# Stick-breaking attention: the off-diagonal running product over pairs of keys, with the pair products on GpSimd

## The chip, the cores and the metric

The kernel runs on one core of one Trainium2 chip. The metric is device time in microseconds (us). A core has a matrix engine (PE, with its weight loads written PEld), a vector engine (DVE), a scalar engine (ACT), GpSimd (POOL) and a queue engine for transfers (SP). Each engine works through its own list of instructions in order; semaphores tie the lists together.

## The reference

Two layers over a sequence of 2048 positions, width 1024, all float32. Layer 0 pools over neighbouring positions and is all dense products. Layer 1 is the one that the change touches: causal stick-breaking attention with 16 heads of size 64.

```python
def stick_breaking_attention(q, k, v):
    # A[t,s] = beta[t,s] * prod_{s<j<t} (1 - beta[t,j]), beta = sigmoid(q.k / sqrt(d))
    for blk in range(S // Q_BLOCK):
        ...
        mask = s_idx < t_idx
        log_keep = jnp.where(mask, jax.nn.log_sigmoid(-logits), 0.0)
        later = lax.cumsum(log_keep, axis=-1, reverse=True) - log_keep
        a = jnp.where(mask, jnp.exp(jax.nn.log_sigmoid(logits) + later), 0.0)
        outs.append(jnp.einsum('bhts,bhsd->bhtd', a, v[:, :, :L]))
```

For each query t the weights come from a running product of the keep-factors 1 - beta, taken from the query's own position back to the first key. The kernel doesn't form the weights. It forms the running product itself, R[t,s] = the product of the keep-factors from s to t, and multiplies it by the differences of neighbouring rows of V, which gives the same sum.

## The kernel before

The first half (to about 1390 us) does layer 0 and the projections. Q, K and the differences of V go to DRAM split into two parts (a rounded one and the rest), so that PE works at float32 accuracy in its fast format.

The second half is the attention. The sequence is cut into four blocks of 512. The work is a list of slots in the order `for c in 3..0: for h in 0..15: for kc in c..0`: query block c, head h, key block kc. A slot with kc = c is a diagonal slot; the others are off-diagonal, 96 in all. Each slot has four steps j, one for each 128 queries, so query block c = 3 has 256 steps, c = 2 has 192, c = 1 has 128 and c = 0 has 64, and the off-diagonal slots 384. One step runs through these functions:

- `front` (L718, L719): two PE products give the logits of 128 queries against 512 keys in a PSUM tile `psl`. ACT turns them into keep-factors (L722), in one of four fixed buffers `kap`. On a diagonal slot only (j + 1) x 128 keys count, and POOL sets the upper triangle to 1 (L724, a select).
- `scan` (L729): DVE runs the product from the last key to the first, into one of twelve `pp` buffers. It starts from 1 on the diagonal and from the carry of the slot before otherwise, which is the first column of that slot's `pp`.
- `turn` (L743 to L747): PE transposes four 128 x 128 pieces, one from each of the slot's four `pp`, into a PSUM tile `psa` (two buffers). ACT copies it in the rounded format (L746), DVE subtracts to get the rest (L747); both go into a tile `at`.
- `gather` (L755, L756): PE multiplies both parts with the differences of V and adds up in `pso`. At the end of a head `os` takes the result (L760, L761); for every second head ACT adds a bias (L767) and POOL multiplies by the gate (L768).

The main loop is a pipeline written out by hand: at iteration n it issues the turn of step n - 6, the front and the scan of step n, a share of other work, and the gather of step n - 8. A turn needs all four `pp` of its slot.

The other work is a generator of dense products (`piecewise`, L784 to L788), a few PE matmuls per step. Beside c = 3 it is `gate_z`, 32 products, each finished by a DVE multiplication (L825), an ACT sigmoid (L827) and a POOL multiplication (L828). Beside c = 2, 1 and 0 it is `post` of the block before: 8 output projections, each finished on DVE (L849), ACT (L851) and POOL (L852), then 8 gated additions (L871 on ACT, L874 on DVE, L875 on POOL, L876 on DVE); `pair_up` (L804, L805) splits the attention's results. A scheduler may shift instructions within an engine's list; `keep_in_program_order` pins one.

Of the kernel before, what the change touches and what calls it, by code (L numbers as in the profile page):

```python
# [8 lines left out]
F32 = mybir.dt.float32  # L9
F32R = mybir.dt.float32r  # L10
AF = mybir.ActivationFunctionType
ALU = mybir.AluOpType
AX = mybir.AxisListType

P = 128
# [6 lines left out]
W5 = 512  # L22
# [12 lines left out]
def trunk_kernel(ctx, tc, x, p, a_norm, a_w_in, a_w_group, a_scale, a_w_out, kv_norm, w_kv,  # L35
                 k_norm, b_norm, b_w_in, b_q_norm, b_w_out, ple_w, ple_gate_w, out):
    nc = tc.nc
    V, A, G, T = nc.vector, nc.scalar, nc.gpsimd, nc.tensor
# [105 lines left out]
    with ExitStack() as st:  # L144
# [3 lines left out]
        t2 = st.enter_context(tc.tile_pool(name="t2", bufs=2))  # L148
# [516 lines left out]
    with ExitStack() as st:  # L665
        wpair = st.enter_context(tc.tile_pool(name="wpair2", bufs=6))
        t2 = st.enter_context(tc.tile_pool(name="s2", bufs=2))
        kap = st.enter_context(tc.tile_pool(name="kap", bufs=1))
# [7 lines left out]
        zeros = kap.tile([P, 1], F32, name="zeros")  # L676
        V.memset(zeros, 0.0)
        kcount = [0]

        def load_q(c, h):  # L680
            qa = io.tile([P, W5], F32R, tag="io", name="qa")
            qb = io.tile([P, W5], F32R, tag="io", name="qb")
            rows = qd[c][h // 2][h % 2 * HD : (h % 2 + 1) * HD]
            for l in range(2):
                nc.sync.dma_start(out=f(qa)[l * HD : (l + 1) * HD], in_=rows[:, l])
                nc.sync.dma_start(out=f(qb)[(1 - l) * HD : (2 - l) * HD], in_=rows[:, l])
            return qa, qb
# [23 lines left out]
        def front(st, j):  # L711

            w = (j + 1) * P if st["diag"] else W5
            r0 = W5 - w
            ps = psl.tile([P, W5], F32, tag="psl", name="psl")
            qs = slice(j * P, (j + 1) * P)
            (qa, qb), kk = st["q"], st["k"]
            T.matmul(ps[:, :w], qa[:, qs], kk[:, :w], start=True, stop=False)  # L718
            T.matmul(ps[:, :w], qb[:, qs], kk[:, :w], start=False, stop=True)  # L719
            kp = kaps[kcount[0] % NK]  # L720
            kcount[0] += 1
            A.activation(out=kp[:, r0:], in_=ps[:, :w], func=AF.Sigmoid, scale=-1.0)  # L722
            if st["diag"]:
                G.affine_select(out=kp[:, W5 - P :], in_=kp[:, W5 - P :], pattern=[[-1, P]], compare_op=ALU.is_gt,  # L724
                                fill=1.0, base=0, channel_multiplier=1)

            def scan():
                pp = t2.tile([P, W5], F32, tag="pp", name="pp", bufs=12)
                V.tensor_tensor_scan(out=pp[:, r0:][:, ::-1], data0=kp[:, r0:][:, ::-1],  # L729
                                     data1=zeros.to_broadcast([P, w]),  # L730
                                     initial=1.0 if st["diag"] else st["carry"][j], op0=ALU.mult, op1=ALU.add)
                st["carry"][j] = pp[:, r0 : r0 + 1]
                st["a"].append((pp, r0))

            return scan

        def turn(st, kt):

            j0 = kt if st["diag"] else 0
            pt = psa.tile([P, W5], F32, tag="psa", name="psa")  # L740
            for j in range(j0, 4):
                pp, r0 = st["a"][j]
                T.transpose(pt[:, j * P : (j + 1) * P], pp[:, r0 + kt * P : r0 + (kt + 1) * P], ident)  # L743
            at = t2.tile([P, 2, W5], F32R, tag="at", name="at", bufs=3)
            cs = slice(j0 * P, W5)
            A.copy(out=at[:, 0, cs], in_=pt[:, cs])  # L746
            V.tensor_tensor(out=at[:, 1, cs], in0=pt[:, cs], in1=f(at[:, 0, cs]), op=ALU.subtract)  # L747
            st["at"][kt] = at

        def gather(st, kt):  # L750
            cs = slice((kt if st["diag"] else 0) * P, W5)
            if st["diag"] and kt == 0:
                st["o"].append(pso.tile([P, W5], F32, tag="pso", name="pso"))
            po, at, vv = st["o"][0], st["at"].pop(kt), st["v"]
            T.matmul(po[:, cs], vv[:, kt, :], at[:, 0, cs], start=(st["diag"] and kt == 0), stop=False)  # L755
            T.matmul(po[:, cs], vv[:, kt, :], at[:, 1, cs], start=False, stop=(st["last"] and kt == 3))  # L756
            if st["last"] and kt == 3:
                half, os, c, h2 = st["h"] % 2, st["os"], st["c"], st["h"] // 2
                mine, other = slice(half * HD, (half + 1) * HD), slice((1 - half) * HD, (2 - half) * HD)
                A.copy(out=os[mine], in_=po[other])  # L760
                V.tensor_tensor(out=os[mine], in0=po[mine], in1=os[mine], op=ALU.add)  # L761
                if half:
                    zt = t2.tile([P, W5], F32, tag="zt", name="zt", bufs=1)
                    nc.sync.dma_start(out=zt, in_=zd[c][h2])
                    for j in range(4):
                        js = slice(j * P, (j + 1) * P)
                        A.activation(out=os[:, js], in_=os[:, js], func=AF.Identity, bias=ends[c][:, h2, j : j + 1])  # L767
                    G.tensor_tensor(out=os, in0=os, in1=zt, op=ALU.mult)  # L768
                    outs[c].append(os)
# [127 lines left out]
        def beside(c):  # L897

            if c < NSUB - 1:
                yield from post(c + 1)  # L900
                return
            for cz in range(c, -1, -1):
                yield from gate_z(cz)
# [9 lines left out]
        rate = POSTZ / 64.0  # L913
        LAG_T, LAG_G = 6, 8
        done = set()
        ends = {}

        def begin(i):
            c, h, kc = slots[i]
            if kc == c:  # L920
                if h == 1:
                    ends[c] = load_ends(c)
                os = head["os"] if h % 2 else t2.tile([P, W5], F32, tag="os", name="os", bufs=9)
                head.clear()
                head.update(q=load_q(c, h), carry=[None] * 4, o=[], os=os)
            kk, vv = load_kv(kc, h)
            active[i] = dict(head, c=c, h=h, k=kk, v=vv, diag=kc == c, last=kc == 0, a=[], at={})

        for n in range(4 * len(slots) + LAG_G):
            i2, j2 = divmod(n - LAG_T, 4)  # L930
            if 0 <= i2 < len(slots):
                turn(active[i2], j2)
            i, j = divmod(n, 4)
            scan = None
            if i < len(slots):
                c, h, kc = slots[i]
                if j == 0:
                    if i == 0:
                        begin(0)
                    if i + 1 < len(slots):  # L940
                        begin(i + 1)
                scan = front(active[i], j)
            if scan is not None:
                scan()
            owed += rate
            while owed >= 1.0:
                next(filler, None)
                owed -= 1.0
            i3, j3 = divmod(n - LAG_G, 4)
            if 0 <= i3 < len(slots):  # L950
                gather(active[i3], j3)
                if j3 == 3:
                    st3 = active.pop(i3)
                    c3 = st3["c"]
                    if len(outs[c3]) == 8 and c3 not in done:
                        done.add(c3)
                        for _ in filler:
                            pass
                        if c3:
                            filler = beside(c3 - 1)  # L960
                            rate = POST / (64.0 * c3 - 2 * LAG_G)
                            owed = 0.0
# [31 lines left out]
```

## Time and profile before

| what | value |
|---|---|
| median of 3 runs | 2802.99 us (2802.78 to 2803.59) |
| the profiled execution | 2804.4 us, of which its span is 2802.5 us |
| granted PE clock | 0.996 of full speed |
| PE busy | 2735.2 us (98%) |
| DVE busy | 1899.5 us (68%) |
| ACT busy | 1391.6 us (50%) |
| POOL busy | 932.2 us (33%) |

The profile is one execution. A row of its groups has line, engine, operation, tiles written <- read, shape and count, then the busy time in us, the mean in ns of one, and the idle time of the engine before them with what ended it. A row of its timeline has start in us, duration in us, engine, line, operation. A row of its windows gives for each engine the busy time and the number of instructions in one stretch of time. A row of its waits says who waited for whom, the total in us, how often, and the longest. Matmuls are pipelined, and their ends are modelled.

### The profile page before, as it was taken

Reading aid. Unit: us, or ns where it says so; the run is one execution under the profiler, and the core shown is the slowest. Engines: PE = TensorE matmul, PEld = TensorE weight load, DVE = VectorE, ACT = ScalarE, POOL = GpSimd, SP = SyncE. Lnnn points to the kernel's source line nnn. Section 1 sums busy time; section 2 is a strip of 40 time slices with the busy share of each in tenths; the row PEclk is TensorE's granted clock in tenths of the full one; section 3 lists DMA queues with packets and bytes.
Section 4 is the critical chain, followed back from the end, with each engine's and each line's share of the span. In section 5 each row is a group of like instructions: output and inputs, shape, how many; then the busy total and the mean of one; then the engine's idle time right before and its main releaser. Section 6 shows DMA issues by size and latency. Waiting matters only on the chain. (4 is left out here: it accounts for less than half of the span.)

```text
span 2802.5 us, 40461 instructions
## 1 busy us (share of the span) xinstructions
PE 2735.2 (98%) x13731; PEld 2264.3 (81%) x13731; DVE 1899.5 (68%) x2573; ACT 1391.6 (50%) x2801; POOL 932.2 (33%) x949
## 2 busy tenths in 40 slices
PE   8999999999999999999899999999999999999999
PEld 7878888888888888888678888887878778878877
DVE  5655635455355544555299999999999998886642
ACT  5435533445234542345265556556666665554431
POOL 2464337542475425643211111211211122223220
PEclk9999999999999999999999999999999999999999
DMA  8754696647955488455657575555555565668765
GB/s 274 248 180 162 223 321 221 198 161 250 342 172 202 167 270 297 147 183 187 198 183 233 166 224 167 165 170 181 164 168 165 174 188 181 199 183 256 248 204 162
DMA packets 335844, 573.29 MB, mean 205 GB/s; under 512 B 32462, under 2 KB 166638, under 8 KB 335636
## 3 DMA queue, kind: packets, MB, share of 16 engines
q1 hardware_dynamic: 328632, 561.19, 62.2%
q10 hardware_dynamic: 7004, 9.51, 1.1%
q8 instruction: 109, 1.79, 0.3%
q14 instruction: 99, 0.81, 0.1%
HBM read 430.01 MB, written 132.19 MB: 201 GB/s over the span
## 5 line engine op out<-in xcount | busy, mean ns | idle before, releaser
L473 PE MATMUL psd<-wpair,x 128*128 128x512 f32 x2304 | 545.0, 393 | 0.6 <-DVE x L179 0.5
L746 ACT CAST at<-psa 128x512 fp32r<-128x512 f32 (+3 forms) x640 | 333.1, 522 | 407.0 <-PE psa L743 402.0
L729 DVE TENSOR_TENSOR_SCAN pp<-kap,pp,zeros 128x512 f32<-128x512 f32 x384 | 510.8, 1331 | 5.4 <-ACT kap L722 3.2
L473 PEld LDWEIGHTS psd<-wpair,x 128*128 128x128 f32 x2304 | 427.9, 188 | 88.1 <-DVE x L179 1.1
L747 DVE TENSOR_TENSOR at<-psa,at 128x512 fp32r<-128x512 f32 (+3 forms) x640 | 379.1, 594 | 60.1 <-ACT at L746 57.6
L743 PE MATMUL psa<-ident,pp 128*128 128x128 f32 x2176 | 347.1, 275 | 25.7 <-DVE at L747 21.0
L722 ACT ACTIVATE kap<-psl 128x512 f32<-128x512 f32 (+3 forms) x640 | 343.5, 538 | 17.0 <-PE psl L719 8.4
L743 PEld LDWEIGHTS psa<-ident,pp 128*128 128x128 f32 x2176 | 263.5, 141 | 102.8 <-DVE at L747 45.7
L724 POOL TENSOR_SCALAR_AFFINE_SELECT kap<-kap 128x128 f32<-128x128 f32 x256 | 89.6, 351 | 628.0 <-ACT kap L722 522.6
L718 PE MATMUL psl<-kk,qa 128*128 128x512 f32 (+3 forms) x640 | 281.2, 439 | 4.1 <-ACT vr L511 3.4
L729 DVE TENSOR_TENSOR_SCAN pp<-kap,zeros 128x128 f32<-128x128 f32 (+3 forms) x256 | 213.5, 835 | 40.8 <-POOL kap L724 37.4
L756 PE MATMUL pso<-at,vv 128*128 128x512 f32 (+3 forms) x640 | 235.2, 368 | 0.0
L719 PE MATMUL psl<-kk,qb 128*128 128x512 f32 (+3 forms) x640 | 234.7, 367 | 0.0
L755 PE MATMUL pso<-at,vv 128*128 128x512 f32 (+3 forms) x640 | 232.4, 363 | 1.3 <-ACT at L746 1.2
L130 PE MATMUL psd<-xp,wpair 128*128 128x512 f32 x512 | 201.8, 395 | 0.3 <-ACT xp L232 0.3
L131 PE MATMUL psd<-xp,wpair 128*128 128x512 f32 x512 | 200.5, 392 | 0.0
L132 PE MATMUL psd<-xp,wpair 128*128 128x512 f32 x512 | 200.3, 391 | 0.0
L107 POOL TENSOR_TENSOR wpair<-wraw,wpair 128x512 fp32r<-128x512 f32 x99 | 141.1, 1431 | 82.5 <-ACT wpair L105 52.5
L112 DVE SCALAR_TENSOR_TENSOR wpair<-wraw,gains,wpair 128x512 fp32r<-128x512 f32 x192 | 149.0, 796 | 25.8 <-ACT wpair L111 25.0
L111 ACT ACTIVATE wpair<-wraw,gains 128x512 fp32r<-128x512 f32 x192 | 133.9, 718 | 30.9 <-PE psd L473 27.3
L755 PEld LDWEIGHTS pso<-at,vv 128*128 128x128 f32 x640 | 120.4, 188 | 28.2 <-ACT at L746 2.6
L756 PEld LDWEIGHTS pso<-at,vv 128*128 128x128 f32 x640 | 120.5, 188 | 24.9
(206 smaller groups left out, 5408.8 us busy)
## 6 DMA issues: line engine op xcount, KB each, us to landing
kk<-kd SPq DMA_DIRECT2D x320, 128.0 KB
vv<-vd SPq DMA_DIRECT2D x160, 256.0 KB
wraw<-in_w_kv_dram SPq DMA_DIRECT2D x128, 256.0 KB
wpair<-wzd SPq DMA_DIRECT2D x64, 512.0 KB
wpair<-wod SPq DMA_DIRECT2D x64, 512.0 KB
wpair<-wgd SPq DMA_DIRECT2D x64, 512.0 KB
wpair<-wu SPq DMA_DIRECT2D x48, 512.0 KB
wpair<-wi SPq DMA_DIRECT2D x36, 512.0 KB
```

The lines of the kernel that those rows point to most:

```text
L130: T.matmul(ps, wst(units, kt, 0, c0), acts[kt][:, 0], start=(kt == order[0]), stop=False)
L131: T.matmul(ps, wst(units, kt, 0, c0), acts[kt][:, 1], start=False, stop=False)
L473: T.matmul(pss2[i], ck["x2"][kt][:, xh, tk], wst(ws, kt, wh, 0, W5), start=(kt == 0 and xh == 0 and wh == 0), stop=(kt == KT - 1 and wh == 1))
L718: T.matmul(ps[:, :w], qa[:, qs], kk[:, :w], start=True, stop=False)
L719: T.matmul(ps[:, :w], qb[:, qs], kk[:, :w], start=False, stop=True)
L722: A.activation(out=kp[:, r0:], in_=ps[:, :w], func=AF.Sigmoid, scale=-1.0)
L729: V.tensor_tensor_scan(out=pp[:, r0:][:, ::-1], data0=kp[:, r0:][:, ::-1], data1=zeros.to_broadcast([P, w]), initial=1.0 if st["diag"] els ...
L743: T.transpose(pt[:, j * P : (j + 1) * P], pp[:, r0 + kt * P : r0 + (kt + 1) * P], ident)
L746: A.copy(out=at[:, 0, cs], in_=pt[:, cs])
L747: V.tensor_tensor(out=at[:, 1, cs], in0=pt[:, cs], in1=f(at[:, 0, cs]), op=ALU.subtract)
L755: T.matmul(po[:, cs], vv[:, kt, :], at[:, 0, cs], start=(st["diag"] and kt == 0), stop=False)
L756: T.matmul(po[:, cs], vv[:, kt, :], at[:, 1, cs], start=False, stop=(st["last"] and kt == 3))
```

## The change

On off-diagonal slots the running product no longer visits every key. POOL first multiplies neighbouring keep-factors (even key times the odd key above it), which gives 256 products of two keys (P). DVE scans these, from the last pair to the first, and so gets the running product at the even keys. POOL then multiplies each odd key's factor by the running product at the next even key, which fills in the odd keys (O). The `pp` buffers become fixed, two columns longer: a constant 1 in the last column serves as the factor of a pair that holds only the carry, so the scan has 257 entries and writes the carry behind the last key. The P of a step is issued with its front, before its scan; the O of a step is issued one iteration later, after the next front, and pinned there. Diagonal slots keep their scan. Each POOL product has 256 elements for each of 128 partitions, at a step of two elements.

```diff
+        NP = 12
+        pps = [kap.tile([P, W5 + 2], F32, name=f"pp{i}") for i in range(NP)]
+        for pp in pps:
+            G.memset(pp[:, W5 + 1 :], 1.0)
...
+            pp = pps[(kcount[0] - 1) % NP]
+            pp2, m = pp.rearrange("q (n e) -> q n e", e=2), W5 // 2
+            if not st["diag"]:
+                kp2 = kp.rearrange("q (n e) -> q n e", e=2)
+                G.tensor_tensor(out=pp2[:, 0:m, 1], in0=kp2[:, :, 0], in1=kp2[:, :, 1], op=ALU.mult)
+
             def scan():
-                pp = t2.tile([P, W5], F32, tag="pp", name="pp", bufs=12)
-                V.tensor_tensor_scan(out=pp[:, r0:][:, ::-1], data0=kp[:, r0:][:, ::-1],
-                                     data1=zeros.to_broadcast([P, w]),
-                                     initial=1.0 if st["diag"] else st["carry"][j], op0=ALU.mult, op1=ALU.add)
+                if st["diag"]:
+                    V.tensor_tensor_scan(out=pp[:, r0:W5][:, ::-1], data0=kp[:, r0:][:, ::-1],
+                                         data1=zeros.to_broadcast([P, w]), initial=1.0, op0=ALU.mult, op1=ALU.add)
+                else:
+                    V.tensor_tensor_scan(out=pp2[:, :, 0][:, ::-1], data0=pp2[:, :, 1][:, ::-1],
+                                         data1=zeros.to_broadcast([P, m + 1]), initial=st["carry"][j],
+                                         op0=ALU.mult, op1=ALU.add)
+                    odd.append(lambda: tc.keep_in_program_order(G.tensor_tensor(
+                        out=pp2[:, 0:m, 1], in0=kp2[:, :, 1], in1=pp2[:, 1:, 0], op=ALU.mult)))
...
                 scan = front(active[i], j)
+            while odd:
+                odd.pop(0)()
             if scan is not None:
                 scan()
```

1 line of the change is left out of this document (added).

## The prediction

> **What bounds the kernel now.** I read the page, then the windows by stage, then the timeline of one step, then the waits. The profiled execution took 2804.4 us and its span is
>
> ```profile
> span 2802.5 us, 40461 instructions
> ```
>
> so 1.9 us lie around the span; the runs' median, 2802.99 us, is 1.4 us under it. I work in differences and put them on the median. About 0.2% (5.6 us) is the least that a measurement of this kernel can tell from no change.
>
> The change acts in the attention part alone. I cut the trace at the first sigmoids of the query blocks c = 3, 2 and 1, which have 256, 192 and 128 steps by the loops; c = 0 has no off-diagonal slot.
>
> ```profile
> core 0: us, PE busy (x) PEld busy (x) DVE busy (x) ACT busy (x) POOL busy (x), PEclk, DMA share, GB/s
> 1393.60:1893.80 500.20, 490.97 (x2672) 407.33 (x2672) 470.10 (x561) 298.01 (x593) 95.87 (x102) 1.00 0.60 187
> 1893.80:2250.90 357.10, 346.18 (x1921) 284.61 (x1919) 342.64 (x434) 228.55 (x470) 63.15 (x89) 1.00 0.57 171
> 2250.90:2514.80 263.90, 255.07 (x1412) 212.54 (x1411) 232.31 (x304) 158.25 (x339) 58.02 (x88) 1.00 0.62 189
> ```
>
> PE is busy for 98, 97 and 97% of the three stages, DVE for 94, 96 and 88%, and POOL for 19, 18 and 22%. Per head (16 in each stage) a stage has 31.26, 22.3 and 16.5 us. The PE idle time that a lighter DVE could give back is small: 500.2 - 491.0, 357.1 - 346.2 and 263.9 - 255.1, together 28.9 us. That caps the gain near 1%, however much DVE time is saved. One off-diagonal step of c = 3 on PE and DVE:
>
> ```profile
> 1602.07 0.60 PE L743 MATMUL psa<-ident,pp 128*128 128x128 f32 x4
> ...
> 1602.43 0.48 PE L718 MATMUL psl<-kk,qa 128*128 128x512 f32 x1
> ...
> 1603.19 0.60 ACT L722 ACTIVATE kap<-psl 128x512 f32<-128x512 f32 x1
> ...
> 1604.49 0.47 PE L718 MATMUL psl<-kk,qa 128*128 128x512 f32 x1
> ```
>
> ```profile
> 1603.09 1.27 DVE L729 TENSOR_TENSOR_SCAN pp<-kap,pp,zeros 128x512 f32<-128x512 f32 x1
> 1604.28 0.66 DVE L747 TENSOR_TENSOR at<-psa,at 128x512 fp32r<-128x512 f32 x1
> 1604.86 1.27 DVE L729 TENSOR_TENSOR_SCAN pp<-kap,pp,zeros 128x512 f32<-128x512 f32 x1
> ```
>
> PE needs 1604.49 - 1602.43 = 2.06 us a step, DVE 1604.86 - 1603.09 = 1.77 us. DVE falls behind only where other work joins it, and then PE waits with its transposes for a psa buffer:
>
> ```profile
> PE psa L743 <- DVE at L747: 18.3, 37, 1.3
> ```
>
> ```profile
> PEld psa L743 <- DVE at L747: 40.7, 73, 1.7
> ```
>
> These are the waits of the three stages. The first row counts time in which no matmul ran; the second counts the weight load of the same transposes, part of it beside matmuls still in flight. What DVE costs PE lies between 18 and 41 us; I take 30.
>
> **What goes and what comes.** On DVE, each of the 384 off-diagonal scans goes from 512 keys to 257.
>
> ```profile
> L729 DVE TENSOR_TENSOR_SCAN pp<-kap,pp,zeros 128x512 f32<-128x512 f32 x384 | 510.8, 1331 | 5.4 <-ACT kap L722 3.2
> L747 DVE TENSOR_TENSOR at<-psa,at 128x512 fp32r<-128x512 f32 x427 | 286.6, 672 | 28.3 <-ACT at L746 27.0
> L729 DVE TENSOR_TENSOR_SCAN pp<-kap,zeros 128x512 f32<-128x512 f32 x48 | 58.5, 1218 | 6.5 <-POOL kap L724 6.3
> L729 DVE TENSOR_TENSOR_SCAN pp<-kap,zeros 128x384 f32<-128x384 f32 x48 | 46.4, 966 | 3.5 <-POOL kap L724 0.9
> L729 DVE TENSOR_TENSOR_SCAN pp<-kap,zeros 128x256 f32<-128x256 f32 x48 | 35.9, 748 | 13.5 <-POOL kap L724 13.4
> ...
> L729 DVE TENSOR_TENSOR_SCAN pp<-kap,zeros 128x128 f32<-128x128 f32 x48 | 20.6, 429 | 3.2 <-POOL kap L724 3.2
> ...
> L805 DVE TENSOR_TENSOR og<-os,og 128x512 fp32r<-128x512 f32 x22 | 14.9, 682 | 0.0
> L876 DVE TENSOR_TENSOR sg<-sg,x 128x512 f32<-128x512 f32 x16 | 13.4, 840 | 10.5 <-POOL sg L875 10.5
> ```
>
> From 128 to 512 keys a scan grows by 789 ns, 2.05 ns a key, so 257 keys cost 429 + 129 x 2.05 = 693 ns: DVE gets 384 x (1.331 - 0.69) = 246 us. No row has a scan at a step of two elements. If the skipped elements were paid for it would cost 1.22 us again, the row of 512; if a step cost nothing, 0.69. I take 0.69, since the cost follows the key count in four rows.
>
> On POOL come 768 products of 256 keys at a step of two: P, neighbouring keep-factors in pairs, before the scan; and O, the values between, after it. Nearest rows:
>
> ```profile
> L390 POOL TENSOR_TENSOR us<-us 128x521 f32<-128x521 f32 x16 | 16.9, 1054 | 1.1
> ...
> L179 POOL TENSOR_TENSOR kpair<-kraw,kpair 128x256 fp32r<-128x256 f32 x8 | 6.0, 751 | 23.5 <-ACT kpair L178 23.5
> ```
>
> Bounds of p, the price of one product: the 256-wide row gives 0.75 us. The 521-wide row, whose two inputs lie in one tile as P's do, runs faster; with the fixed 0.21 us worked out below it gives 0.21 + 256 x (1.054 - 0.21)/521 = 0.62. If the 256 strided keys were paid like the 512 that they span, p would be the 1.29 us of the L875 row below. I take 0.75, the row of the same size.
>
> The Trainium skill, page "GPSIMD Engine Reference", section "Performance pitfalls for Q7 kernels", says that reads cost about half as much again once step times element size exceeds 8 bytes, and here the step is exactly 8. By that rule there is no surcharge and p stays 0.75; with the surcharge p would be an estimated 1.1. No run here shows it.
>
> POOL's idle share would hold 384 x 1.5 = 576 us of products in the 1121 us of the stages if POOL worked freely beside DVE. It doesn't:
>
> ```profile
> 1561.63 3.77 POOL L828 TENSOR_TENSOR zr<-zr,sgz 128x512 f32<-128x512 f32 x1 [10.45 <-issue]
> 1561.67 1.27 DVE L729 TENSOR_TENSOR_SCAN pp<-kap,pp,zeros 128x512 f32<-128x512 f32 x1
> ...
> 1563.05 1.27 DVE L729 TENSOR_TENSOR_SCAN pp<-kap,pp,zeros 128x512 f32<-128x512 f32 x1
> ...
> 1564.82 1.66 DVE L729 TENSOR_TENSOR_SCAN pp<-kap,pp,zeros 128x512 f32<-128x512 f32 x1
> ```
>
> ```profile
> 2383.66 0.29 POOL L724 TENSOR_SCALAR_AFFINE_SELECT kap<-kap 128x128 f32<-128x128 f32 x1 [0.93 <-ACT kap L722]
> 2383.69 0.28 DVE L747 TENSOR_TENSOR at<-psa,at 128x128 fp32r<-128x128 f32 x1
> 2383.92 1.29 POOL L875 TENSOR_TENSOR sg<-sg,x 128x512 f32<-128x512 f32 x1
> 2383.98 1.77 DVE L729 TENSOR_TENSOR_SCAN pp<-kap,zeros 128x256 f32<-128x256 f32 x1
> ```
>
> A scan and a POOL product exclude each other; the subtraction L747, which reads PSUM, is left alone. The product at 1561.63 stood until the second scan had ended at 1564.32 and then took 1.08 us, 0.21 less than 1.29: its head passes beside the scan. The scan at 2383.98 (256 keys, 0.69 of its own) ended at 2385.75, so it began in earnest at 2385.06, when the product had held it off for 1.14 of its 1.29 us: the last 0.15 is free. A step's P, O and scan therefore take turns: 2p + 0.69 - 0.15 - 0.21 = 1.83 us at p = 0.75.
>
> Per head, POOL and the scans then share: 12, 8 or 4 off-diagonal steps of 1.83; the diagonal scans, 1.22 + 0.97 + 0.75 + 0.43 = 3.37; four selects L724 of 0.29, 1.16; the 512-wide products at 1.14 each (c = 3: two of L828 and half a one of L768, 2.85; otherwise half a one each of L768, L852, L875, 1.71); and outside c = 3 the DVE operations with two SBUF inputs, half a one of L876 (0.34) and 22/48 of L805 (0.31). Sums: c = 3 22.0 + 7.4 = 29.4 of 31.26 us, 94%; c = 2 14.6 + 6.9 = 21.5 of 22.3, 97%; c = 1 7.3 + 6.9 = 14.2 of 16.5, 86%. That is nearly DVE's load of today. PE stays the bound, by little.
>
> **The new chain and its waits.** A sigmoid ends at 1603.79; the transposes that need its row first come three steps behind their own step's, at 1602.07 + 3 x 2.06 = 1608.25, 4.46 us later (the built program keeps PE's order: nearly all transposes still stand behind five later fronts). With POOL in step, P takes 0.75, O of the step before follows at once, the scan gets in at 1.35 and ends at 2.04; POOL takes the next P at 2.06 and this O after it, done at 2.06 + 1.5 = 3.56. Slack: 0.9 us. The scan now waits for P at the head of DVE's queue, with the next subtraction L747 behind it, which holds a psa buffer; it needs no more than the turn above. O waits for the scan at the head of POOL's queue, with the selects and L828, L852, L875 behind it. The twelve memsets and the fixed buffers cost nothing: POOL idles there, and twelve buffers stood there before.
>
> Where the slack fails: in about half of the 16 cases of L875 in c = 2 and 1, POOL's list reaches it right behind a step's P, while the multiplication L874 that it needs stands in DVE's list behind the same step's scan. POOL then stands for 0.69 + 0.67 us (L874 taken as L747's row) and works for 1.29, 1.75 beyond the slack. In c = 2, with 3% to spare, that is 4 x 1.75 = 7 us, and 1.29 - 0.9 = 0.4 for each of the other twelve, 5 us. In c = 1 spare time takes it up, 3 us. At the end of each head in c = 3 an L828 stands before the last O, some 0.2 late, 3 us. New waits: 18 us. A lighter DVE returns the 30. Sum: -30 + 18 = -12, so 2803 - 12 = **2791 us**.
>
> **The rivals.** *POOL becomes the bound* (slower). Against it stands the row of 0.75; for it, that no row has strided operands on POOL and that the spare share is thin. The turn outgrows PE's time in c = 2 from 8 x (2p + 0.33) + 6.9 = 22.3, p = 0.80; in c = 3 from 0.83; in c = 1 from 1.03. At p = 0.95 the turn is 2.23 us: c = 3 gains 26.8 + 7.4 - 31.3 = 2.9 us a head, c = 2 2.4, times 16 = +85: 2888 us. At p = 1.29, with turns of 2.91, it is +177, +126 and +33: 3139 us. A scan of 1.22 us would do the same at p = 0.75: a turn of 2.36, +71 in c = 3 and +56 in c = 2, 2930 us.
>
> The Trainium skill, page "SBUF — State Buffer", section "Who interferes with whom", gives the rule behind this rival: a Vector instruction with two SBUF inputs and a GpSimd instruction that reads SBUF lock each other out. The 3.77 us of L828 agree.
>
> *The new waits eat the gain*: p = 0.75, but in c = 1 too the spare time takes up nothing: 7 + 5 us there as well, in place of 3, and with L828's 3 it is 27 us against the 30. The time stays at 2800 us; a few more late products put it a little above 2803. For it: DVE's queue is in order, and it now waits for POOL at every step.
>
> *Both products run like the 521-wide row*: p = 0.62, a turn of 1.57, 84% in c = 3; new waits all but vanish, -29: 2774 us. This is the low end of my forecast's mechanism.
>
> **How the numbers follow.** Forecast (PE stays the bound, 2774 to 2797 us): 0.45. New waits eat the gain (2797 to 2815): 0.17, of which 0.10 lies within 0.2% and 0.07 above. POOL the bound (2815 up): 0.38. Faster 0.45, same 0.10, slower 0.45. The range runs from 2772 to 2885 (p = 0.94); it leaves out the dearer prices, 0.14, and a little below.
>
> **What would show it.** In the profile after: scans off the diagonal between 0.7 and 1.3 us, since a scan that an O holds off counts as busy; products near 0.75 us where no scan is in the way; POOL 80% or more busy in c = 3 for the same reason, DVE between 70 and 90%; PE at 98% or more; the wait of L743's transposes for DVE under 10 us. The forecast is wrong if the products take 0.8 us or more on their own, if PE's share falls in c = 3 and c = 2, and if PE's transposes wait for POOL.

## The result and the profile after

| | before | after |
|---|---|---|
| median | 2803.29 us (2802.78 to 2803.89, 4 runs) | 2851.32 us (2847.73 to 2856.89, 4 runs) |
| ratio | 1 | 1.0173, interval 1.0161 to 1.0186 |
| the profiled execution | 2804.4 us | 2847.73 us |
| PE busy | 2735.2 us | 2746.7 us |
| DVE busy | 1899.5 us | 1858.1 us |
| POOL busy | 932.2 us | 1510.0 us |

The change costs 48 us where a gain of 12 was forecast. The loss lies where the change acts. These are the windows of the three stages after; the columns are the busy times of PE, PEld, DVE, ACT and POOL, each with its count, then PE's granted clock, the share of DMA and GB/s:

```profile
1390.70:1912.00 521.30, 499.06 (x2683) 411.61 (x2682) 446.75 (x561) 299.80 (x595) 375.95 (x498) 0.99 0.55 180
1912.00:2287.30 375.30, 350.28 (x1913) 287.77 (x1912) 332.06 (x433) 227.76 (x469) 263.62 (x344) 0.98 0.52 162
2287.30:2559.50 272.20, 256.74 (x1417) 212.53 (x1417) 227.03 (x307) 158.20 (x341) 155.53 (x218) 1.00 0.59 186
```

c = 3 is 21.1 us longer, c = 2 18.2 and c = 1 8.3, together 47.6. PE's idle time in them, 28.9 us before, is 22.2 + 25.0 + 15.5 = 62.7 now: 33.8 of the 47.6. Its busy time grew by the other 13.8, and the granted clock reads 0.99 and 0.98 in the first two. The trace after has six short stretches of 3.41 us in the three stages in which the granted clock is one half, where the trace before has one. These are two of the six, in c = 2:

```profile
2165.30:2168.70 3.40, 3.40 (x13) 2.81 (x12) 3.36 (x5) 0.77 (x2) 3.08 (x4) 0.51 0.76 247
2213.10:2216.50 3.40, 3.40 (x13) 2.82 (x13) 2.91 (x4) 1.48 (x4) 2.63 (x4) 0.50 0.79 230
```

Five stretches more, at half their 3.41 us, are an estimated 8.5 of the 13.8 us. Why the clock falls there is not shown. DVE's busy time in c = 3 fell by 23 us only, of the 192 x 0.64 = 123 that the prediction's price for the scan gives there. The groups say why:

```profile
L744 DVE TENSOR_TENSOR_SCAN pp<-pp,pp,zeros 128x257 f32<-128x257 f32 x384 | 442.3, 1152 | 97.5 <-POOL pp L735 95.4
...
L747 POOL TENSOR_TENSOR pp<-kap,pp 128x256 f32<-128x256 f32 x384 | 333.8, 869 | 1.9 <-DVE pp L744 1.9
L735 POOL TENSOR_TENSOR pp<-kap 128x256 f32<-128x256 f32 x384 | 287.2, 748 | 198.2 <-ACT kap L726 196.0
```

L744 is the scan off the diagonal: 257 keys in place of 512, and 1.152 us in place of 1.331. L735 is P, L747 is O. DVE also stands 95.4 us at P. In front of PE, the wait of the transposes (L743 before, L760 now) for DVE's subtraction (L747 before, L764 now) grew from 18.3 to 45.6 us, and in their weight loads from 40.7 to 57.8, in the waits of the three stages:

```profile
DVE pp L744 <- POOL pp L735: 95.4, 138, 2.4
PEld psa L760 <- DVE at L764: 57.8, 61, 2.5
PE psa L760 <- DVE at L764: 45.6, 53, 2.4
...
PEld psa L760 <- POOL pp L747: 7.8, 18, 1.1
...
PE psa L760 <- POOL pp L747: 1.6, 7, 0.6
```

PE waits little for POOL itself: 1.6 us in which no matmul ran, 7.8 in the weight loads. It waits for DVE, and DVE for POOL.

**A steady step.** Two engines of c = 3 in the timeline, POOL and DVE:

```profile
1640.53 0.86 POOL L747 TENSOR_TENSOR pp<-kap,pp 128x256 f32<-128x256 f32 x1
1640.66 1.28 DVE L744 TENSOR_TENSOR_SCAN pp<-pp,pp,zeros 128x257 f32<-128x257 f32 x1
...
1641.45 0.90 POOL L735 TENSOR_TENSOR pp<-kap 128x256 f32<-128x256 f32 x1
...
1641.86 0.66 DVE L764 TENSOR_TENSOR at<-psa,at 128x512 fp32r<-128x512 f32 x1
...
1642.31 0.85 POOL L747 TENSOR_TENSOR pp<-kap,pp 128x256 f32<-128x256 f32 x1
...
1642.45 1.28 DVE L744 TENSOR_TENSOR_SCAN pp<-pp,pp,zeros 128x257 f32<-128x257 f32 x1
...
1643.51 0.62 POOL L735 TENSOR_TENSOR pp<-kap 128x256 f32<-128x256 f32 x1 [0.34 <-ACT kap L726]
```

P alone takes 0.62 us (the last row), O 0.85; the P at 1641.45 takes 0.90, since a scan is running beside it. O starts right behind P, 0.14 us ahead of the scan that P released. That scan then lasts 1.28 us. DVE's turn is 1642.45 - 1640.66 = 1.79 us, against 1.77 before: what half the keys save, the hold-off takes back.

**The place where PE stands.** Here is the middle of a head of c = 3 in the timeline, POOL first, then DVE, then PE's fronts and one turn:

```profile
1596.78 0.62 POOL L735 TENSOR_TENSOR pp<-kap 128x256 f32<-128x256 f32 x1 [0.54 <-ACT kap L726]
1597.35 0.86 POOL L747 TENSOR_TENSOR pp<-kap,pp 128x256 f32<-128x256 f32 x1
1598.16 1.67 POOL L845 TENSOR_TENSOR zr<-zr,sgz 128x512 f32<-128x512 f32 x1
1599.79 1.28 POOL L785 TENSOR_TENSOR os<-os,zt 128x512 f32<-128x512 f32 x1
1601.03 0.62 POOL L735 TENSOR_TENSOR pp<-kap 128x256 f32<-128x256 f32 x1
```

```profile
1597.88 0.87 DVE L744 TENSOR_TENSOR_SCAN pp<-pp,pp,zeros 128x257 f32<-128x257 f32 x1
1599.00 0.29 DVE L764 TENSOR_TENSOR at<-psa,at 128x128 fp32r<-128x128 f32 x1 [0.25 <-ACT at L763]
1601.68 1.32 DVE L744 TENSOR_TENSOR_SCAN pp<-pp,pp,zeros 128x257 f32<-128x257 f32 x1 [2.39 <-POOL pp L735]
1602.92 0.66 DVE L764 TENSOR_TENSOR at<-psa,at 128x512 fp32r<-128x512 f32 x1
```

```profile
1595.16 0.48 PE L722 MATMUL psl<-kk,qa 128*128 128x512 f32 x1
...
1596.89 0.48 PE L722 MATMUL psl<-kk,qa 128*128 128x512 f32 x1
...
1598.84 0.47 PE L722 MATMUL psl<-kk,qa 128*128 128x512 f32 x1
...
1600.66 0.48 PE L722 MATMUL psl<-kk,qa 128*128 128x512 f32 x1
...
1603.64 0.66 PE L760 MATMUL psa<-ident,pp 128*128 128x128 f32 x4 [1.40 <-DVE at L764]
1604.05 0.48 PE L722 MATMUL psl<-kk,qa 128*128 128x512 f32 x1
```

Two 512-wide products, L845 of the gate and L785 of the attention's result, stand in POOL's list one behind the other, ahead of a P. Together they take 2.9 us. DVE waits 2.39 us at its head for that P; the subtraction behind, which holds a psa buffer, comes out late; PE stands 1.40 us. From front to front the steps take 1.73, 1.95, 1.82 and then 1604.05 - 1600.66 = 3.39 us. The steps up to the stall have the diagonal slot's last turns and its gathers, with fewer pieces and columns than an off-diagonal slot's, so PE goes fast there. L785 comes with every second head. The stretch from a head's twelfth front to its thirteenth, read off PE's timeline in this way (at the second product of each front) for the 16 heads of c = 3, has a mean of 2.85 us after and 2.11 before. The medians are 3.42 against 2.35 in heads with an L785, and 2.16 against 1.79 in the others. In c = 2, where it leads to the next head's first front, the mean is 2.53 against 1.82. So 16 x (0.74 + 0.71) = 23 us of the loss show at this one step of a head. That is where PE stands, and not yet why.

### The profile page after: what moved, and what is told of

Its sections match the earlier page's. It is cut to its first block, busy times and chain, and to the rows that moved or that the text cites. A ratio compares the mean times of both kernels' runs of the same rounds, so it can differ in the third digit from the quotient of the medians.

```text
span 2845.6 us, 41510 instructions
## 1 busy us (share of the span) xinstructions
PE 2746.7 (97%) x13731; PEld 2270.8 (80%) x13731; DVE 1858.1 (65%) x2573; ACT 1391.6 (49%) x2801; POOL 1510.0 (53%) x1729
## 3 DMA queue, kind: packets, MB, share of 16 engines
q8 instruction: 109, 1.79, 0.3%
## 4 chain that ended last, share of the span: by engine, by line
PE 70%; DVE 12%; POOL 7%; issue 4%; ACT 3%; DMA 3%; ACTq 0%; SPq 0%; POOLq 0%; DVEq 0%
PE psd L473 18%; PE psd L131 7%; PE psd L130 7%; PE psd L132 7%; PE psa L760 5%; DVE pp L744 4%; PE psd L803 4%; PE psd L801 4%; PE psd L805 4%; DVE at L764 3%; PE pso L773 2%; PE pso L772 2%; PE psl L723 2%; PE psl L722 2%; POOL pp L735 2%
## 5 line engine op out<-in xcount | busy, mean ns | idle before, releaser
L744 DVE TENSOR_TENSOR_SCAN pp<-pp,pp,zeros 128x257 f32<-128x257 f32 x384 | 442.3, 1152 | 97.5 <-POOL pp L735 95.4
L764 DVE TENSOR_TENSOR at<-psa,at 128x512 fp32r<-128x512 f32 (+3 forms) x640 | 377.4, 591 | 58.3 <-ACT at L763 54.3
L760 PE MATMUL psa<-ident,pp 128*128 128x128 f32 x2176 | 352.3, 277 | 56.9 <-DVE at L764 47.4
L735 POOL TENSOR_TENSOR pp<-kap 128x256 f32<-128x256 f32 x384 | 287.2, 748 | 198.2 <-ACT kap L726 196.0
L760 PEld LDWEIGHTS psa<-ident,pp 128*128 128x128 f32 x2176 | 265.8, 141 | 139.2 <-DVE at L764 61.6
L747 POOL TENSOR_TENSOR pp<-kap,pp 128x256 f32<-128x256 f32 x384 | 333.8, 869 | 1.9 <-DVE pp L744 1.9
L741 DVE TENSOR_TENSOR_SCAN pp<-kap,zeros 128x128 f32<-128x128 f32 (+3 forms) x256 | 229.8, 899 | 37.4 <-POOL kap L728 36.2
```

The costliest lines, as they stand in the source:

```text
L735: G.tensor_tensor(out=pp2[:, 0:m, 1], in0=kp2[:, :, 0], in1=kp2[:, :, 1], op=ALU.mult)
L744: V.tensor_tensor_scan(out=pp2[:, :, 0][:, ::-1], data0=pp2[:, :, 1][:, ::-1], data1=zeros.to_broadcast([P, m + 1]), initial=st["carry"][j ...
L747: odd.append(lambda: tc.keep_in_program_order(G.tensor_tensor(out=pp2[:, 0:m, 1], in0=kp2[:, :, 1], in1=pp2[:, 1:, 0], op=ALU.mult)))
```

## The experiments

All were timed in three rounds; the medians of before beside them lie between 2803.3 and 2803.9 us. For the main ones this is the time from the first front of each query block to the first of the next, in us, read at the second product of a front in their profiled executions (that of the kernel after is the fastest of its four):

| kernel | c = 3 | c = 2 | c = 1 |
|---|---|---|---|
| before | 516.8 | 356.9 | 264.0 |
| after | 534.1 | 376.4 | 272.4 |
| after without O | 511.3 | 350.1 | 263.8 |
| after, short memsets in O's place | 524.6 | 352.5 | 265.0 |
| after, 88 of the 512-wide products on DVE | 529.3 | 362.2 | 267.1 |
| control, one psd | 543.8 | 385.7 | 280.5 |
| the same, zeros in PSUM | 522.7 | 354.8 | 267.9 |
| the same, all 120 of the 512-wide products on DVE | 513.2 | 348.5 | 262.9 |

**What a shorter scan is worth, and what P and O each cost.** The first kernel is the one before with the off-diagonal scan cut to 256 keys and no work on POOL (the other half of the keys is left out).

```diff
-                V.tensor_tensor_scan(out=pp[:, r0:][:, ::-1], data0=kp[:, r0:][:, ::-1],
-                                     data1=zeros.to_broadcast([P, w]),
+                hw = w if st["diag"] else W5 // 2
+                V.tensor_tensor_scan(out=pp[:, r0 : r0 + hw][:, ::-1], data0=kp[:, r0 : r0 + hw][:, ::-1],
+                                     data1=zeros.to_broadcast([P, hw]),
```

> The kernel before, with one thing left out: off the diagonal the scan covers 256 of the 512 keys (the other half of the running product keeps old values), and POOL does nothing new. It asks what a lighter DVE is worth by itself. By the forecast's term it is worth the 30 us that DVE costs PE: 2773 us, at best 2774 less nothing since PE's idle time in the three stages was 28.9 us. If PE's waits before had another cause than DVE's load (the chain of transposes, copies and subtractions itself), it is worth under 10 us: 2795 us or more.

Measured: 2774.86 us (2774.29 to 2776.32), ratio 0.9896 (0.9882 to 0.9911). The 30 us that a lighter DVE was to return are real: 29.

The second is the kernel after without O (the two lines of its product are deleted; the odd keys' values are left out).

> The changed kernel with O left out (the odd keys keep their pair products); P and the scan of 257 stay. Theory of the hold-off: O starts right behind P and keeps the scan out for 0.55 us in every step, so the scan's saving never reaches DVE; without O the scans take about 0.74 us, DVE's waits for P hardly matter, and the time falls below the kernel before, to 2775 to 2790 us. Rival, the chain: what hurts is that the scan waits for P at the head of DVE's queue with the subtraction behind it; P is still there, so the time stays at 2835 us or more.

Measured: 2790.98 us (2789.95 to 2792.63), ratio 0.9954 (0.9939 to 0.9968). That is 1 us above its range. With P alone the change is faster than before; O costs 2851.3 - 2791.0 = 60 us.

The third drops O too, and lets the scan read the even columns of `kap`, so that P is formed but nobody waits for it:

```diff
-                    V.tensor_tensor_scan(out=pp2[:, :, 0][:, ::-1], data0=pp2[:, :, 1][:, ::-1],
-                                         data1=zeros.to_broadcast([P, m + 1]), initial=st["carry"][j],
+                    V.tensor_tensor_scan(out=pp2[:, 0:m, 0][:, ::-1], data0=kp2[:, :, 0][:, ::-1],
+                                         data1=zeros.to_broadcast([P, m]), initial=st["carry"][j],
```

> The kernel after without O, and with P formed on POOL as before but read by nobody: the scan goes over the 256 even columns of the keep-factors themselves, so it needn't wait for P. The odd keys' factors are left out of the product. The version without O took 2790.98 us, the one with neither P nor O 2774.86. Theory W (the 16 us between them are the scan's wait for P, 0.6 us in the chain from sigmoid to scan): 2773 to 2780. Theory L (they come from P and the scan locking each other out): 2786 to 2793.

Measured: 2781.32 us (2779.48 to 2782.61), ratio 0.9920 (0.9905 to 0.9934). It lies between the two ranges, nearer to the wait: of the 16 us, 10 go with the scan's wait for P and 6 with P's work beside the scan. The split is rough, since the scans that wait for P, in the second kernel, take 0.805 us, and those that don't are held off by it for longer. The group of the latter shows that a held-off scan need not cost PE much:

```profile
L744 DVE TENSOR_TENSOR_SCAN pp<-kap,pp,zeros 128x256 f32<-128x256 f32 x384 | 412.9, 1076 | 10.1 <-ACT kap L726 7.0
```

At a mean of 1.08 us they are nearly as long as after, but they stand nowhere (10.1 us of idle time ahead of 384 scans). Step by step from before to after this is -29 + 6 + 10 + 60 = +47 us. These steps lie end to end between the two kernels, so they must add up to the 48, and the sum proves nothing about what each step means.

**Where O does its harm.** One rival was the chain: the scan waits for P, so give it an iteration more (the scan, the turns and the gathers each move back by one).

```diff
-        LAG_T, LAG_G = 6, 8
+        LAG_T, LAG_G = 7, 9
+        held = [None]
...
+            scan, held[0] = held[0], scan
```

> The changed kernel with every scan issued one iteration later, and turns and gathers one iteration later with it, so that P is done before DVE comes to its scan and the subtraction of the step stands in front of the scan. POOL and DVE do the same work. Theory of the hold-off: O, P and scan still take turns at 1.84 us, and the time stays within 10 us of 2850. Rival, the chain: DVE's waits for P (95 us in the three stages) go, and with them PE's; 2800 us or less.

Measured: 2848.17 us (2847.23 to 2849.5), ratio 1.0157 (1.0142 to 1.0172). DVE still stands 106.5 us at P, and PE 44.2 us at DVE. The stretch from the twelfth front to the thirteenth is down to a median of 1.83 us in c = 3, but PE stands at other steps instead. A queue that falls behind is not mended by a longer lead; the chain falls as a cause.

O on DVE (`V.tensor_tensor` in the lambda):

> The changed kernel with O on DVE, issued before the next scan; P stays on POOL. Nothing is left out. Theory of the hold-off: DVE's turn is 0.74 + 0.42 + 0.66 less 0.24 of overlaps, 1.58 us against 1.77 before, and nothing on POOL stands behind P; 2780 to 2795 us, faster than both kernels. Rival, the chain: DVE still waits for P and carries O besides; 2840 us or more.

Measured: 2814.48 us (2811.77 to 2817.56), ratio 1.0036 (1.0023 to 1.0049). It lies between the two ranges. POOL is free of O and 37 us come back, but O takes 0.57 us on DVE in the mean (0.42 in the median), and the change still loses 11.

Next O's place in POOL's queue was kept and its reading taken away: memsets stand where O stood (O's values are left out), first three of 256 columns, then two of 256 and one of 128.

```diff
-                    odd.append(lambda: tc.keep_in_program_order(G.tensor_tensor(
-                        out=pp2[:, 0:m, 1], in0=kp2[:, :, 1], in1=pp2[:, 1:, 0], op=ALU.mult)))
+                    odd.extend([lambda a=a, b=b: tc.keep_in_program_order(G.memset(pp2[:, a:b, 1], 0.5))
+                                for a, b in ((0, 256), (0, 256), (0, 128))])
```

> The changed kernel with O replaced by three memsets of 256 elements on POOL, at O's place, with O's wait for the scan and O's target; the odd keys hold 0.5, which leaves that part of the running product out. POOL is occupied at least as long as by O (about 0.9 us a step against 0.85), but reads no SBUF. Theory of the hold-off: a POOL instruction that reads nothing does not keep the scan out, the scans take 0.74 us, and the time falls to that without O, 2791 us, plus little: under 2805 us. Rival, POOL's queue: what O costs is the POOL time in front of the next P, and the time stays at 2840 us or more.

> The kernel after, with each O replaced by memsets of 256, 256 and 128 columns, about 0.33 + 0.33 + 0.2 = 0.85 us, O's own time alone, where the earlier version of this test had 1.0 us. They read no SBUF. The odd columns are left out of the result. Theory L (the lock is the whole loss that O brings): with scans at 0.75 us the time falls to that of the version without O, 2791, within 8 us. Theory Q (O also costs by its place in POOL's queue, ahead of the next P and the selects): the time stays 20 to 30 us above the version without O, 2811 to 2821, as the longer memsets gave. If the length of the earlier memsets alone was to blame, the wait of PE's transposes for POOL falls from 18.7 us to under 5.

Measured: 2820.43 us (2819.1 to 2821.6) for the longer ones, ratio 1.0061 (1.0044 to 1.0078), and 2812.62 us (2811.71 to 2815.99) for the shorter, ratio 1.0034 (1.0021 to 1.0047). The groups of the shorter ones:

```profile
L744 DVE TENSOR_TENSOR_SCAN pp<-pp,pp,zeros 128x257 f32<-128x257 f32 x384 | 288.7, 752 | 175.8 <-POOL pp L735 174.6
L747 POOL MEMSET pp<- 128x256 f32 x768 | 255.9, 333 | 22.3 <-DVE pp L744 1.2
...
L747 POOL MEMSET pp<- 128x128 f32 x384 | 82.8, 216 | 21.9
```

A step's memsets take 0.333 + 0.333 + 0.216 = 0.88 us, like O's 0.87, but the scan runs in 0.752 us: nothing holds it off. The first time lies between its two ranges, the second in the range of theory Q. Of O's 60 us, 2851.3 - 2812.6 = 39 go with the reading; by the table they lie mostly in c = 2 (24 us).

The other 2812.6 - 2791.0 = 22 can't be put down to the time that O takes in POOL's queue. In the profiled execution about 5 of them lie ahead of the attention, whose first front comes at 1381.4 us here and at 1376.7 without O. By the table 13 lie in c = 3, at a step that is quick in the kernel after. POOL, then PE, in one of its heads:

```profile
1567.44 0.61 POOL L735 TENSOR_TENSOR pp<-kap 128x256 f32<-128x256 f32 x1 [0.43 <-ACT kap L726]
1567.99 0.33 POOL L747 MEMSET pp<- 128x256 f32 x1
1568.27 1.65 POOL L845 TENSOR_TENSOR zr<-zr,sgz 128x512 f32<-128x512 f32 x1
1569.86 0.59 POOL L747 MEMSET pp<- 128x256 f32 x2
```

```profile
1570.50 0.33 PE L760 MATMUL psa<-ident,pp 128*128 128x128 f32 x1 [0.87 <-POOL pp L747]
```

Three instructions in place of one O leave room for an L845 between them, in 15 of the 16 heads. The memsets behind it come 1.65 us late, and the transpose that needs their row waits for them. From the tenth front of a head to the eleventh the median is 3.04 us, against 1.95 in the kernel after and in the one without O. So 39 us is a lower figure for the reading, and 22 an upper one for O's time in the queue. The guess that the length of the earlier memsets was to blame was wrong too: PE's wait for POOL, 18.7 us with them, is 17.1 with the shorter ones.

**The lock with all work present.** The scan has two inputs in SBUF, the factors and `zeros`, one column read over and over. In the next three kernels this column lies in PSUM. PSUM has no room left for it, so psd gets one buffer in place of two, and the generator of dense products pauses three turns ahead of each. A control has these edits without the move.

```diff
-        psd = st.enter_context(tc.tile_pool(name="psd2", bufs=2, space=bass.MemoryType.PSUM))
+        psd = st.enter_context(tc.tile_pool(name="psd2", bufs=1, space=bass.MemoryType.PSUM))
...
-        zeros = kap.tile([P, 1], F32, name="zeros")
+        psz = st.enter_context(tc.tile_pool(name="psz", bufs=1, space=bass.MemoryType.PSUM))
+        zeros = psz.tile([P, 1], F32, name="zeros")
```

The control, with `zeros` in SBUF:

> The control for the next kernel: the changed kernel with one psd buffer in place of two, and three empty turns of the generator ahead of each dense product so that PE does not wait for the buffer. Nothing is left out. Either theory: near the changed kernel, 2840 to 2880 us, with scans off the diagonal held off as before (mean over 1.1 us).

The kernel after with `zeros` in PSUM:

> As the control, and the freed PSUM bank holds the column of zeros that the scan adds, so that the scan reads one SBUF operand in place of two. All of P, O and the scan is there. Theory of the hold-off: the scan and POOL's products no longer exclude each other; scans of 0.75 to 0.85 us, DVE's turn 1.3 us, and 40 to 70 us less than the control, 2780 to 2810 us. Rival, POOL's queue: 1.46 us of POOL work and the wait for P are as before; within 10 us of the control.

The kernel before with the same edits:

> The kernel before with the same three edits: one psd buffer, three empty turns, zeros in PSUM. Scans of 512 keys off the diagonal that POOL cannot hold off, near 1.27 us each in place of the mean of 1.33. Theory of the hold-off: little is at stake in the kernel before, since POOL is 20% busy; 2790 to 2810 us, and the changed kernel with zeros in PSUM is at least as fast. Rival: as fast as before or slower, and faster than the changed kernel with zeros in PSUM by 40 us.

Measured: control 2882.36 us (2878.21 to 2888.69), ratio 1.0284 (1.0267 to 1.0300); `zeros` in PSUM 2819.04 us (2817.09 to 2819.15), ratio 1.0054 (1.0039 to 1.0069); before with them 2807.71 us (2805.55 to 2808.98), ratio 1.0013 (1.0004 to 1.0022). The scans of the control, then those with `zeros` in PSUM:

```profile
L745 DVE TENSOR_TENSOR_SCAN pp<-pp,pp,zeros 128x257 f32<-128x257 f32 x384 | 451.3, 1176 | 99.8 <-POOL pp L736 98.7
```

```profile
L746 DVE TENSOR_TENSOR_SCAN pp<-pp,pp,zeros 128x257 f32<-128x257 f32 x384 | 286.7, 747 | 164.3 <-POOL pp L737 160.9
```

One operand's place takes 0.43 us off each scan and 63 us off the kernel, with every product still formed. It is not that a scan is quicker with PSUM: with `zeros` in SBUF and memsets in O's place it took 752 ns above. The lock is shown as the larger part of the loss: measured from the last kernel, the pair products cost 2882.4 - 2807.7 = 75 us with it in this arrangement and 11 without it. The arrangement itself is dear, for the control is 31 us slower than the kernel after, 2 us above its range; how much the move of `zeros` alone would give the kernel after was not measured, since PSUM has no room for it there. The kernel with `zeros` in PSUM is 9 us above its range, and it was to be at least as fast as the kernel before with the same edits, which it isn't. There, too, the scan gets shorter, from 1331 to 1271 ns:

```profile
L731 DVE TENSOR_TENSOR_SCAN pp<-kap,pp,zeros 128x512 f32<-128x512 f32 x384 | 487.3, 1271 | 4.6 <-ACT kap L724 2.2
```

**The rest, POOL's queue.** In the first of the next three kernels all 120 512-wide products (L785, L845, L869, L892) move to DVE. The other two were meant to have the same four edits, but L845 (L828 before), 32 products that all stand beside c = 3, stays on POOL in them, and only the other 88 move. The edit of L845; the others replace G by V in the same way:

```diff
-                G.tensor_tensor(out=zr, in0=zr, in1=sg, op=ALU.mult)
+                V.tensor_tensor(out=zr, in0=zr, in1=sg, op=ALU.mult)
```

On top of `zeros` in PSUM:

> The kernel with zeros in PSUM (2819.04 us, 11 us above its own before), and the 512-wide POOL products of the gate, the projections and the additions (L785, L845, L869, L892, 120 in all) moved to DVE. Theory Q (what is left of the loss is POOL's queue: P and O late behind 1.1 to 1.3 us of other work): 5 to 20 us are gained, 2799 to 2814; under 2798 it would beat both kernels. Rival (what is left is the scan's wait for P and the chain, whatever else POOL does): no change or a few us more, 2817 to 2830, since DVE takes some 80 us of new work with two SBUF inputs.

In the kernel after, with the lock in place:

> The kernel after (two psd, zeros in SBUF, so with the lock), and only the 512-wide POOL products of the gate, the projections and the additions (120 in all) moved to DVE. Theory A (two separate losses, the lock 60 us and POOL's queue 25 us): about 25 us are gained, 2820 to 2832, and the interval from step 11 to 12 in c = 3 falls from 2.85 us toward 2.1 while scans stay near 1.15 us. Theory B (with the lock the turn is what counts, so POOL's other work is indifferent or DVE's added operations lengthen the turn): 2842 to 2870.

In the kernel before with `zeros` in PSUM, without pair products:

> The counterpart of the fastest version without the pair products: the kernel before, with its scan of 512 keys, zeros in PSUM, one psd, and the same 120 products on DVE. Theory A (the fastest version needs the pair products, since only they make room on DVE): slower than before by 10 us or more, 2815 to 2850. Rival (moving the gate away from POOL brings the gain by itself): 2790 to 2800, no slower than the version with pairs (2794.47).

Measured: 2794.47 us (2792.73 to 2795.9), ratio 0.9966 (0.9955 to 0.9978); 2821.59 us (2820.43 to 2823.93), ratio 1.0068 (1.0053 to 1.0083); 2805.06 us (2802.65 to 2808.43), ratio 1.0008 (0.9999 to 1.0018). The move of the 88 alone gives the kernel after 30 us back, though its scans are as long as ever and DVE has more to do:

```profile
L744 DVE TENSOR_TENSOR_SCAN pp<-pp,pp,zeros 128x257 f32<-128x257 f32 x384 | 441.7, 1151 | 68.4 <-POOL pp L735 66.7
```

The stretch that took 3.39 us above takes 2.22 in the same head here, with its L845 still on POOL and only L785 gone; its mean falls from 2.85 to 2.39 us in c = 3 and from 2.53 to 2.13 in c = 2. By the table 5 us come back in c = 3, 14 in c = 2 and 5 in c = 1, where all of the products move. In c = 2 the parts overlap: without the reading 24 of its us come back, without the 512-wide products 14, and only 26 are there by the kernel without O. A queue that is held off falls behind where rare long work joins it, and either cure gives it room. With the lock gone, the move of all 120 takes 2819.0 - 2794.5 = 25 us off, more than the 5 to 20 expected: 9.5 in c = 3 (522.7 to 513.2) and 6 in c = 2. With both mended, the pair products are worth 2805.1 - 2794.5 = 11 us. The kernel before, at 2805.1 in neither of its two ranges, gains nothing that can be told from the move of its 88 (2807.7 without it). In its profile no instruction waits for the products of L828, so little is to be had from them, but a version with all 120 on DVE and without the pair products was not timed. With that left open, the fastest version does need the pair products.

O on DVE with `zeros` in PSUM:

> Zeros in PSUM as before, and O on DVE (0.41 us alone). Theory L: what the version with O on DVE lost against before (2814.5 us, +11) came from P and the DVE operations holding each other off. The scan is now free of it, O (two SBUF inputs) isn't: half of it goes, 2795 to 2808. Rival (DVE's queue is the loss: O stands ahead of the scans and both wait for P): no change, 2812 to 2822.

Measured: 2830.57 us (2828.25 to 2831.67), ratio 1.0094 (1.0077 to 1.0110), above both ranges. Half of the loss did not go, so O and P holding each other off is not shown as the cause; how much of it is the single psd and the pauses was not measured apart.

**A version faster than both.** The fastest kernel so far, with the room for `zeros` taken from pso (one buffer in place of two), so that psd and the generator are as in the kernel after:

> The fastest version (zeros in PSUM, the 120 products on DVE, 2794.47 us) gives up a psd bank and three empty turns of the generator for the zeros. Here the bank is taken from pso (one in place of two), and psd and the generator are as before. If the change of psd costs what it cost the kernel before (4 us) or the kernel after (31 us), 4 to 15 us come back: 2780 to 2790. Rival: with one pso the first gather of a head waits until the result of the head before is copied out, 64 heads by up to 1.5 us, of which PE covers most: 2795 to 2830.

Measured: 2788.64 us (2787.66 to 2790.4), ratio 0.9948 (0.9932 to 0.9965): 15 us under before and 63 under after. Among its waits in the attention:

```profile
PE pso L773 <- DVE os L779: 8.6, 24, 0.8
...
PE psa L761 <- DVE at L765: 5.4, 11, 1.0
```

The wait for DVE's subtraction is down to 5.4 us, and PE stands 8.6 us for the single pso.

## Why the prediction was wrong

**The bound and the 30 us: right.** PE bounds the kernel, and a scan of half the keys alone gives 29 us.

**The prices: right.** P was to be 0.75 and O 0.75; they are 0.62 and 0.85, 1.47 together against 1.5. That the sum came out is in part luck, for one was put too high and the other too low. The scan was to be 0.69 and is 0.75 (the row of 747 ns). DVE's and POOL's turn was to be 1.83 us and comes to 1.47 + 0.75 - 0.36 = 1.86; the trace has 1.79. So the rival in which products at 0.80 us or more make POOL the bound is not what happened. A step of 8 bytes brought no surcharge: by the rule of the Trainium skill, page "GPSIMD Engine Reference", section "Performance pitfalls for Q7 kernels", there was to be none at this step, and the 0.62 us of P agree. O's 0.85 is 0.10 above the contiguous row; whether its step or its two tiles are the reason was not tried.

**"A lighter DVE returns the 30": the first step that failed.** The same part of the text priced the scan with its hold-off, in a turn of 1.83 us against DVE's 1.77 before, and said that this "is nearly DVE's load of today". A DVE that is as loaded as before returns nothing. The 30 us were booked at the scan's own price, while the scan's price in company was known. The runs put the hold-off's part at 39 us or more (reading O against memsets) and at 63 in the control's arrangement (`zeros` moved). The Trainium skill, page "SBUF — State Buffer", section "Who interferes with whom", has the rule that a Vector instruction with two SBUF inputs and a GpSimd instruction that reads SBUF lock each other out, and that a Vector instruction with one input in SBUF, outside its two-port modes, or a GpSimd instruction that only writes, is free of it. The runs agree with all three: scans of 1152, 747 and 752 ns.

**"New waits: 18 us": the second, in size and in place.** The runs have 10 us for the scan's wait for P and 6 for P's work. With `zeros` in PSUM, and so without the lock, the pair products still lost 11 us where the first experiment had 29 to win; if the 29 hold there too, the new waits are an estimated 40, and the move of the 512-wide products took 25 of them away. The sums of load per head (94, 97 and 86%) were a mean over a head, and the slack of 0.9 us came from a step at PE's pace of 2.06. But the steps are not alike. On diagonal steps POOL idles for ACT's sigmoids (126.3 us ahead of the selects in the three stages after), and on the steps with the diagonal slot's turns and gathers PE goes at 1.73 to 1.95 us, about the 1.79 to 1.84 of the turn, so there is no slack just where the 512-wide products come. The text had an L828 (now L845) "some 0.2 late, 3 us" at the end of a head in c = 3, and spread L768 (now L785) as half a product per head. The trace has both in one gap ahead of a P, and PE idle for 1.40 us. The 12 us of c = 2 were near: the move of its 512-wide products gave 14 with the lock and 6 without. That the wait for P holds the subtraction and a psa buffer was named rightly.

**The rivals.** "The new waits eat the gain" has the mechanism that came nearest, at 2800 us or a little above it; the measured loss is larger, since the lock took the gain as well. The measured 2851 us lie inside the stated range, but by luck: that part of it stood for POOL as the bound, with products at 0.80 us or more. That the forecast of 2791 is the time of the version without O is a chance of the sum, but it says where the miss lies: in what O costs.

**The marks that were named.** Scans between 0.7 and 1.3 us: seen. POOL 80% busy in c = 3: it is 375.95/521.30 = 72%. DVE between 70 and 90%: 86%. PE at 98% or more and the wait for DVE under 10 us: 499.06/521.30 = 96%, and 45.6 us. Of the signs that the forecast is wrong, PE's falling share came; PE waiting for POOL came in a small part only (1.6 us, and 7.8 in the weight loads), because the wait goes through DVE.

## What to carry to other kernels

Before work is moved to GpSimd to relieve VectorE, look whether the two read SBUF at the same time, and book what is saved at the price in company, once; an operand moved to PSUM, even a constant column, can take the lock away. A mean share of load says little of in-order queues: write out the queue's list over one whole period, find where rare long instructions fall ahead of something short that others wait for, and compare with the pace of just those steps. Here an engine that was 72% busy held up the one that sets the time.

## What the runs showed of the hardware

- A single column of zeros, read again and again as the second input, acts as a second SBUF input of the scan: with it in PSUM the scan of 257 keys is 747 ns in place of 1176 beside GpSimd's products; the scan of 512 in the kernel before went from 1331 to 1271.
- A GpSimd memset of the same length as O leaves the scan alone (752 ns).
- Two GpSimd products of one size and step differ: 0.62 us with both inputs in one tile (P), 0.85 with the inputs in two tiles (O). Whether the tiles are the reason was not tried.
- The granted clock was one half for 3.41 us at a time: six times in the three stages after, once before, and not once in the kernel after with `zeros` in PSUM. What sets it off was not tried.
